# RWKV heads on one core: both triangular masks in one operation, token shift shared with ScalarE, key norms in two halves, some steps in another place

## The chip, the core and the metric

One NeuronCore of a Trainium2 chip runs the whole program. Its engines are TensorE (PE; PEld is its weight load), VectorE (DVE), ScalarE (ACT), GpSimd (POOL) and SyncE (SP, which issues most DMAs). Each engine works through its own list of instructions in the order written, and waits at an instruction until the semaphores that it names have been raised. The metric is device time in microseconds (us), lower is better.

## What is computed

Two model blocks run one after the other on 256 tokens of width 1024. The first has two layers of feed-forward, mixer, feed-forward; the second has attention, a pooling mixer and two mixtures of experts and is not touched. The change lies in the RWKV half of the first block's mixer, 8 heads of 64, once in each layer:

```python
def token_shift(p, mu):
    prev = jnp.pad(p, ((0, 0), (1, 0), (0, 0)))[:, :-1]
    return p + mu * (prev - p)

def rwkv7_group(p, mu, ...):
    p = token_shift(p, mu)
    r, k, v, w_d, a_d, g_d = jnp.split(p, [o1, o2, o3, o4, o5], axis=-1)
    log_w = -jax.nn.softplus(-(w0 + jnp.tanh(w_d) @ w_lora_up).astype(f32)) - 0.5
    decay = jnp.exp(-jnp.exp(log_w))
    a = jax.nn.sigmoid((a0 + a_d @ a_lora_up).astype(f32))
    kk = heads(k * k_k)
    kk = kk * lax.rsqrt(jnp.maximum(jnp.sum(kk * kk, axis=-1, keepdims=True), 1e-24))
    k_h = heads(k.astype(f32) * (1.0 + (a - 1.0) * k_a.astype(f32)))
    y = rwkv7_scan(r_h, heads(decay), k_h, v_h, -kk, kk * a_h)
    ...

def step(state, inp):          # of rwkv7_scan, over the tokens
    sa = jnp.einsum('bhvk,bhk->bhv', state, a_t)
    state = state * w_t[:, :, None, :] + sa[..., None] * b_t[:, :, None, :] + v_t[..., None] * k_t[:, :, None, :]
    return state, jnp.einsum('bhvk,bhk->bhv', state, r_t)
```

## The kernel before

Nothing is scheduled automatically: the order of the Python code is the order on every engine. Activations lie with features on the partitions and 256 tokens along the row. A weight slab of 1 MB comes by DMA, is cut into a high half (ScalarE, L111) and a remainder (VectorE, L117), and a projection of 128 features is `linear_half` (L607): 8 times three matmuls, high weights by high input (L530), high weights by low input (L531), low weights by high input (L532), 24 in all. The third needs what L117 made. `W.next()` hands out the weights of one such unit and at the same moment writes the L111 and L117 of the unit two places further on into the lists of ScalarE and VectorE; `cuts(3)` does so for up to three units at once.

In `mix_body` the scan over tokens is done in chunks of 64 by matmuls. It has these parts.

- `elementwise(hp)` (L800) is a generator for the pair of head blocks hp (0 or 1). Its steps, cut by `yield`: key projection, first half; key projection, second half, with the token shift of the keys and their squares (L819); receptance projection, first half; second half, then the norms of the keys (matmuls L829, `rsqrt` with its power on GpSimd, L595, tile nk), the decay matmuls L838 with the activations L845 to L862 and the scan L851, and the shift of r; then the matmuls L783 that spread nk over the partitions, and the products kn, AR, BK up to bon (L890); value projection in two halves; last a matmul with bon (L902), for hp 0 after four small matmuls of `warm` (L523).
- `shift` (L767) makes p from the projection (L771), the difference d of neighbours (L773) and p + mu d (L776, once for each half of 128 features).
- `matrices(q)` (L914) works on one block of two heads: products L931, masks L943 and L946 (strictly upper part into G or Gk, upper part with diagonal into R), the first step of an inverse on GpSimd (L967, L968: tile Tt), transposes L955 and L957 with ScalarE's copies L958 to L963, products L973 and transposes L979 with ScalarE's copies L975 and L981, transposes L986 with copies L988 into Tm, then ten rounds in which PE (L1005) and VectorE (L1011 to L1017) take turns, and the rest of the scan.
- `lockstep` (L1206) advances two `matrices` generators by a step each per round, and between rounds takes steps from a third generator that fills in projections. AT1 (L422) lists the rounds after which a fill step is taken: `[0, 0, 1, 1, 2, 2, 3, 4, ...]`. For the first pair the fill is `elementwise(1)` followed by `ret_qk`, and all of `elementwise(0)` runs ahead of it (L1233 to L1237).

PSUM has 8 banks: `bank()` hands out four in turn, `abank()` the other four. A matmul that starts on a bank waits until the last reader of that bank's tile from four calls earlier has finished. In `matrices` the calls of two heads in step are: L931 of the first head two banks, of the second head two, L955 one each, L973 and L979 two each, L986 one each. So L986 of the first head takes the bank that its own L973 filled and that ScalarE's L975 reads, and L986 of the second head takes the bank that the first head's L979 filled and L981 reads.

Of the kernel before, what the change touches and what calls it, by code (L numbers as in the profile page):

```python
# [18 lines left out]
P = 128  # L19
T = 256  # L20
# [313 lines left out]
def _c1():  # L334
# [4 lines left out]
    i, t64 = j % 64, q[None, :]  # L339
    parts = {"strict": i < t64, "incl": i <= t64, "level1": (t64 == i + 1) & (i % 2 == 0), "eye": i == t64}  # L340
    for m in (2, 4, 8, 16, 32):
# [79 lines left out]

AT1 = [0, 0, 1, 1, 2, 2, 3, 4, 14, 15, 17, 18]  # L422
AT2 = [0, 1, 2, 3, 4, 5, 6, 7, 8, 9, 10, 11, 14, 15, 17, 99]
# [9 lines left out]
def body(ctx, tc, nc, A, out):  # L433
# [153 lines left out]
    def rsqrt(out, src, scale, eps, work, floor=None):  # L587

        n = src.shape[-1]
        v = work.tile([P, 16], F32, name="nv", bufs=1)[:, :n]  # L590
# [150 lines left out]
    def mix_body(l, xs, nxt, mx):  # L741
# [11 lines left out]

        Gs = [mat.tile([P, 4, 64], F32, name=f"G{i}") for i in range(2)]
        Qs = [mat.tile([P, 4, 64], F32, name=f"Q{i}") for i in range(2)]
# [11 lines left out]
        def shift(pool, name, blk, pb, **kw):  # L767

            p = ew.tile([P, 2, T + 1], F32, name="p")
            nc.gpsimd.memset(p[:, :, 0:1], 0.0)  # L770
            nc.vector.tensor_tensor(p[:, :, 1:], two(pb), by2(rr), op=OP.mult)  # L771
            d = ew.tile([P, 2, T], F32, name="d")
            nc.vector.tensor_tensor(d, p[:, :, :T], p[:, :, 1:], op=OP.subtract)  # L773
            s = pool.tile([P, 2, T], F32, name=name, **kw)
            for j in range(2):
                nc.vector.scalar_tensor_tensor(s[:, j, :], d[:, j, :], vec("shift_mu", l, blk + j), p[:, j, 1:],  # L776
                                               op0=OP.mult, op1=OP.add)
            return s
# [21 lines left out]
        def elementwise(hp):  # L800
# [30 lines left out]
            nk = ew.tile([P, 8], F32, name="nk")  # L831
            rsqrt(nk, pk[:, :8], None, None, ew, floor=1e-24)

# [80 lines left out]
        def matrices(q):  # L914
            hp, i = divmod(q, 2)
            S = H[hp]
            AR, BK, ec, v = S["AR"][:, :, i], S["BK"][:, i], S["ec"][:, i], S["v"][:, i]
            G, Q = Gs[i], Qs[i]
            lo, hi = slice(0, 64), slice(64, P)
# [16 lines left out]
            for w in range(2):  # L936
                nc.gpsimd.tensor_copy(vx[:, :, 1 - w], vw[:, :, w])
            Gk = tile_([P, 4, 64], "Tm")
            R = tile_([P, 4, 2, 64], "R")
            pgs = [p.rearrange("p (t w x e) -> p t w x e", t=2, w=2, x=2) for p in pgs]  # L940
            for dst, r, w in ((G, lo, 0), (G, hi, 1), (Gk, lo, 1), (Gk, hi, 0)):
                for s in range(2):
                    nc.vector.tensor_tensor(dst[r, 2 * s:2 * s + 2], pgs[s][r, :, w, 0],  # L943
                                            cst["strict"][r, None, :].to_broadcast([64, 2, 64]), op=OP.mult)
            for s in range(2):
                nc.vector.tensor_tensor(R[:, 2 * s:2 * s + 2], pgs[s][:, :, :, 1],  # L946
                                        cst["incl"][:, None, None, :].to_broadcast([P, 2, 2, 64]), op=OP.mult)
            yield
# [17 lines left out]
            Tm = tile_([P, 4, 64], "Tm")  # L966
            nc.gpsimd.tensor_tensor(Tt, G, cst["level1"][:, None, :].to_broadcast([P, 4, 64]), op=OP.mult)  # L967
            nc.gpsimd.tensor_tensor(Tt, Tt, cst["eye"][:, None, :].to_broadcast([P, 4, 64]), op=OP.add)  # L968
            yield
            pz = abank()  # L970
            for n, (s, t) in enumerate(ST):
                for a, b in ((lo, hi), (hi, lo)):
                    nc.tensor.matmul(pz[a, n * 64:(n + 1) * 64], Gk[b, n, :], Vt[b, t, 64 * s:64 * s + 64],  # L973
                                     start=(n == 0), stop=(n == 3), skip_group_check=True)
# [16 lines left out]
            for lev in range(5):  # L991
# [1583 lines left out]
```

## Time and profile before

| | us |
|---|---|
| time, median of 3 (lowest, highest) | 2116.79 (2116.5, 2120.3) |
| profiled execution, its own time | 2116.78 |
| its span, first to last instruction | 2115.0 |
| PE busy in the span | 2016.1 (95%) |
| VectorE, ScalarE, GpSimd busy | 1067.3, 803.0, 284.9 |

The mixer of layer 0 lies at about 204 to 412 us, that of layer 1 at about 806 to 1014. A row of the timeline gives the start, the time until the last of its merged instructions ended, engine, line, operation, what it writes and reads, the count, and in brackets how long the engine had been idle before and who ended that. The granted clock (PEclk) is 1.00 at TensorE's upper level of 2.4 GHz and 0.50 at its lower of 1.2. Ends of matmuls are modelled, so starts are the firmer numbers.

### The profile page before, as it was taken

The page shows a single profiled execution, that of the slowest core. Times are in us where ns is not written, and L with a number is a line of the kernel's source. Part 1 is how long each engine was busy: PE and PEld are TensorE (multiplying, and loading weights), DVE is VectorE, ACT ScalarE, POOL GpSimd, SP SyncE. Part 2 cuts the span into 40 slices and gives each one's busy share as a digit, 9 for nine tenths or more (in the row PEclk, how much of TensorE's full clock was granted, in tenths as well). Part 3 has the DMA queues.
Part 4 walks back from the last instruction along what each step waited for, and adds up shares of the span by engine and source line. Part 5 has one row for each costly group of instructions (what it writes and reads, how often), then busy time and mean ns, then how long its engine had stood idle before and what let it go on. Part 6 is the DMA issues. An engine that isn't in the chain of part 4 may idle for free. (4 is left out here: it accounts for less than half of the span.)

```text
span 2115.0 us, 39279 instructions
## 1 busy us (share of the span) xinstructions
PE 2016.1 (95%) x16724; PEld 1692.6 (80%) x16724; DVE 1067.3 (50%) x1680; ACT 803.0 (38%) x1306; POOL 284.9 (13%) x376
## 2 busy tenths in 40 slices
PE   8999999999999999899999998999999898999996
PEld 8999888899999999878999997997444398864442
DVE  5555764555565556754656567645211266441112
ACT  5444442454454445332444454443111244421111
POOL 3111221111121112221111122300000012000000
PEclk9999999999999999999999999999999999999998
DMA  6445321145545554210544443447999935389995
GB/s 257 185 180 183 129 80 61 61 170 189 187 154 199 190 188 170 81 61 22 214 170 183 180 152 115 180 147 308 416 421 421 404 131 208 131 342 420 421 421 246
DMA packets 63499, 442.98 MB, mean 209 GB/s; under 512 B 6993, under 2 KB 7761, under 8 KB 10705
## 3 DMA queue, kind: packets, MB, share of 16 engines
q1 hardware_dynamic: 60704, 433.30, 53.2%
q10 hardware_dynamic: 1744, 3.90, 0.6%
q0 software_dynamic: 864, 3.15, 0.5%
q8 instruction: 136, 2.23, 0.4%
q14 instruction: 51, 0.41, 0.1%
HBM read 439.27 MB, written 1.05 MB: 208 GB/s over the span
## 5 line engine op out<-in xcount | busy, mean ns | idle before, releaser
L117 DVE TENSOR_TENSOR w<-raw,w 128x1024 fp32r<-128x1024 f32 (+1 forms) x428 | 521.1, 1242 | 228.8 <-ACT w L111 228.5
L530 PE MATMUL pb<-xh,w 128*128 128x256 f32 x2032 | 588.7, 290 | 4.1 <-ACT w L111 3.3
L532 PE MATMUL pb<-xh,w 128*128 128x256 f32 x2032 | 582.2, 287 | 8.1 <-DVE w L117 7.9
L531 PE MATMUL pb<-xl,w 128*128 128x256 f32 x2032 | 582.0, 286 | 7.0 <-DVE xl L1408 4.6
L111 ACT ACTIVATE w<-raw 128x1024 fp32r<-128x1024 f32 (+1 forms) x438 | 443.8, 1046 | 197.7 <-PE pb L532 108.7
L532 PEld LDWEIGHTS pb<-xh,w 128*128 128x128 f32 x2032 | 395.2, 194 | 11.4 <-DVE w L117 11.3
L531 PEld LDWEIGHTS pb<-xl,w 128*128 128x128 f32 x2032 | 395.5, 195 | 10.7 <-DVE xl L1408 5.1
L530 PEld LDWEIGHTS pb<-xh,w 128*128 128x128 f32 x2032 | 395.4, 195 | 10.2 <-ACT w L111 3.8
L532 PE MATMUL ab<-hh,w 128*128 128x256 f32 x704 | 197.9, 281 | 0.0
L530 PE MATMUL ab<-hh,w 128*128 128x256 f32 x704 | 197.9, 281 | 0.0
L531 PE MATMUL ab<-hl,w 128*128 128x256 f32 x704 | 196.3, 279 | 0.0
L2247 PE MATMUL pb<-raw,turn 128*64 128x512 f32 x712 | 175.5, 596 | 0.0
L663 POOL TENSOR_TENSOR h<-sg,gu 128x256 f32<-128x256 f32 x88 | 80.9, 920 | 610.2 <-ACT sg L661 610.2
L530 PEld LDWEIGHTS ab<-hh,w 128*128 128x128 f32 x704 | 132.5, 188 | 0.2 <-issue 0.2
L531 PEld LDWEIGHTS ab<-hl,w 128*128 128x128 f32 x704 | 132.6, 188 | 0.0
L532 PEld LDWEIGHTS ab<-hh,w 128*128 128x128 f32 x704 | 132.2, 188 | 0.0
L2247 PEld LDWEIGHTS pb<-raw,turn 128*64 128x64 f32 x712 | 53.5, 137 | 96.2 <-issue 94.4
L659 DVE TENSOR_TENSOR gu<-pb,rr 128x512 f32<-128x512 f32 x88 | 60.7, 691 | 127.5 <-PE pb L532 121.3
L661 ACT ACTIVATE sg<-gu 128x256 f32<-128x256 f32 x88 | 36.7, 418 | 207.7 <-DVE gu L659 207.7
L2251 ACT ACTIVATE s<-pb 128x512 f32<-128x512 f32 x32 | 19.1, 597 | 199.2 <-PE pb L2247 199.2
L2278 DVE SCALAR_TENSOR_TENSOR ol<-pb,ws,ol 128x512 fp32r<-128x512 f32 x16 | 12.0, 751 | 147.7 <-ACT ol L2277 147.7
L2273 PE MATMUL pb<-raw,h 128*64 128x512 f32 x368 | 85.1, 593 | 0.0
(558 smaller groups left out, 3125.5 us busy)
## 6 DMA issues: line engine op xcount, KB each, us to landing
raw<-in_wpack_dram SPq DMA_DIRECT2D x353, 1024.0 KB, 6.3
w<-in_wpack_dram SPq DMA_DIRECT2D x44, 1024.0 KB, 16.5
x<-in_wpack_dram SPq DMA_DIRECT2D x13, 1024.0 KB, 17.7
gb<-in_vecs_dram POOLq DMA_DIRECT2D x6, 512.0 KB, 7.4
C<-in_c_dram SPq DMA_DIRECT2D x1, 1041.0 KB, 15.5
xin<-in_x_dram SPq DMA_DIRECT2D x2, 512.0 KB, 5.2
mem<-in_mem_dram ACTq DMA_DIRECT2D x1, 1024.0 KB, 9.5
out_dram<-xout SPq DMA_DIRECT2D x4, 256.0 KB, 2.1
```

The source lines that it names most:

```text
L111: self.nc.scalar.activation(h, src, AF.Copy)
L117: (self.nc.gpsimd if pool else self.nc.vector).tensor_tensor(lo, src, h.bitcast(F32), op=OP.subtract)
L530: nc.tensor.matmul(o, wh, xh, start=first, stop=False, skip_group_check=True)
L531: nc.tensor.matmul(o, wh, xl, start=False, stop=False, skip_group_check=True)
L532: nc.tensor.matmul(o, wl, xh, start=False, stop=last, skip_group_check=True)
L659: nc.vector.tensor_tensor(gu, two(pb), rr[:, None, :].to_broadcast([P, 2, T]), op=OP.mult)
L661: nc.scalar.activation(sg, gu[:, 0, :], AF.Silu)
L663: nc.gpsimd.tensor_tensor(h, sg, gu[:, 1, :], op=OP.mult)
L2247: nc.tensor.matmul(o, x_e, w[:, k, :], start=(c == 0), stop=(c == KD - 1), skip_group_check=True)
L2251: nc.scalar.activation(s, pb, AF.Copy)
L2273: nc.tensor.matmul(pb[64 * n:64 * n + 64], h[:, 2 * r + k, :], w[:, k, n * 512:(n + 1) * 512], start=(r == 0 and k == 0), stop=(r == 1 and ...
L2278: V_.scalar_tensor_tensor(o[:, 1], pb, wss[e], o[:, 0].bitcast(F32), op0=OP.mult, op1=OP.subtract)
```

## The change

- `shift`: VectorE's difference d is gone. ScalarE writes d = (1 - mu) p, one activation for each half of 128 features, and VectorE adds mu times the neighbour. The factors 1 - mu are made once at the start by GpSimd.
- `matrices`: one VectorE operation per bank of 512 columns multiplies with both masks side by side; its result GR replaces G, Gk and R. Where 10 operations stood for a head block, 2 stand now. GpSimd's first step on Tt takes its input in two instructions of 64 partitions in place of one of 128.
- The keys' norms: `rsqrt` is called for the two token halves apart.
- The first key projection of `elementwise(1)` is issued ahead of the last step of `elementwise(0)`, and the two fill steps of round 2 move to round 3, the later two by a round each.

```diff
-    parts = {"strict": i < t64, "incl": i <= t64, "level1": ...
+    parts = {"both": np.concatenate([i < t64, i <= t64], axis=1), "level1": ...
-AT1 = [0, 0, 1, 1, 2, 2, 3, 4, 14, 15, 17, 18]
+AT1 = [0, 0, 1, 1, 3, 3, 4, 5, 14, 15, 17, 18]
...
+    vmu = b1.tile([P, 28], F32, name="vmu")
+    nc.gpsimd.tensor_scalar(vmu, vcol[:, mu:mu + 28], -1.0, 1.0, op0=OP.mult, op1=OP.add)
...
-            nc.vector.tensor_tensor(d, p[:, :, :T], p[:, :, 1:], op=OP.subtract)
+            for j in range(2):
+                i = 14 * l + blk + j
+                nc.scalar.activation(d[:, j, :], p[:, j, 1:], AF.Copy, scale=vmu[:, i:i + 1])
...
-                nc.vector.scalar_tensor_tensor(s[:, j, :], d[:, j, :], vec("shift_mu", l, blk + j), p[:, j, 1:],
+                nc.vector.scalar_tensor_tensor(s[:, j, :], p[:, j, :T], vec("shift_mu", l, blk + j), d[:, j, :],
                                                op0=OP.mult, op1=OP.add)
...
-            rsqrt(nk, pk[:, :8], None, None, ew, floor=1e-24)
+            for t in range(2):
+                rsqrt(nk[:, 4 * t:4 * t + 4], pk[:, 4 * t:4 * t + 4], None, None, ew, floor=1e-24)
...
-            for dst, r, w in ((G, lo, 0), (G, hi, 1), (Gk, lo, 1), (Gk, hi, 0)):
-                for s in range(2):
-                    nc.vector.tensor_tensor(dst[r, 2 * s:2 * s + 2], pgs[s][r, :, w, 0],
-                                            cst["strict"][r, None, :].to_broadcast([64, 2, 64]), op=OP.mult)
+            both = cst["both"].rearrange("p (x e) -> p x e", x=2)[:, None].to_broadcast([P, 4, 2, 64])
             for s in range(2):
-                nc.vector.tensor_tensor(R[:, 2 * s:2 * s + 2], pgs[s][:, :, :, 1],
-                                        cst["incl"][:, None, None, :].to_broadcast([P, 2, 2, 64]), op=OP.mult)
+                nc.vector.tensor_tensor(GR[:, s].rearrange("p t w x e -> p (t w) x e"),
+                                        pgs[s].rearrange("p (c x e) -> p c x e", c=4, x=2), both, op=OP.mult)
...
-            nc.gpsimd.tensor_tensor(Tt, G, cst["level1"][:, None, :].to_broadcast([P, 4, 64]), op=OP.mult)
+            for w, r in enumerate((lo, hi)):
+                nc.gpsimd.tensor_tensor(Tt[r], GA[r, :, w], cst["level1"][r, None, :].to_broadcast([64, 4, 64]), op=OP.mult)
...
         together(e0, ret_v(), 7)
+        e1 = elementwise(1)
+        next(e1)
         for _ in e0:
             pass
-        lockstep([steps(matrices(0)), steps(matrices(1))], chained(elementwise(1), qk_steps), AT1)
+        lockstep([steps(matrices(0)), steps(matrices(1))], chained(e1, qk_steps), AT1[1:])
```

Place A, where `elementwise(0)` ends. On PE, of before, the last value projection of `elementwise(0)` is followed by these (L523 is `warm`, L902 the matmul with bon, L931 the first products of the two head blocks, L530 to L532 the key projection of `elementwise(1)`; "..." leaves out the equal rows):

```order
L523 LDWEIGHTS identb
L523 MATMUL pb<-identb 128x512
...
L902 MATMUL pb<-r_2740,bones 128x512
L931 MATMUL ab<-AR,BK 128x128 x16
L530 MATMUL pb<-xh,w 128x256
L531 MATMUL pb<-xl,w 128x256
L532 MATMUL pb<-xh,w 128x256
```

The same place of after:

```order
L533 MATMUL pb<-xh,w 128x256
L534 MATMUL pb<-xl,w 128x256
L535 MATMUL pb<-xh,w 128x256
...
L526 LDWEIGHTS identb
L526 MATMUL pb<-identb 128x512
...
L907 MATMUL pb<-r_2746,bones 128x512
L936 MATMUL ab<-AR,BK 128x128 x16
```

The 24 matmuls of the first key projection, which stood behind L902 and L931, stand ahead of `warm` and of the matmul with bon.

On VectorE at the same place, of before (L890 makes bon; the two L117 are the remainders for the two key projections of `elementwise(1)`; L771 to L776 the value shift; then masks):

```order
L890 SCALAR_TENSOR_TENSOR r_2740<-r,vcol,k 128x256 x2
L117 TENSOR_TENSOR w<-raw,w 128x1024 x2
L771 TENSOR_TENSOR p<-pb,rr 128x2x256
L773 TENSOR_TENSOR d<-p 128x512
L776 SCALAR_TENSOR_TENSOR v<-d,vcol,p 128x256 x2
L903 TENSOR_TENSOR r_2740<-pb,v 128x512
L943 TENSOR_TENSOR G_2338<-ab,C_94 64x128 x4
...
L946 TENSOR_TENSOR R_2854<-ab,C_94 128x256 x2
L117 TENSOR_TENSOR w<-raw,w 128x1024 x3
```

and of after:

```order
L895 SCALAR_TENSOR_TENSOR r_2746<-r,vcol,k 128x256 x2
L117 TENSOR_TENSOR w<-raw,w 128x1024 x2
L773 TENSOR_TENSOR p<-pb,rr 128x2x256
L780 SCALAR_TENSOR_TENSOR v<-p,vcol,d 128x256 x2
L117 TENSOR_TENSOR w<-raw,w 128x1024
L908 TENSOR_TENSOR r_2746<-pb,v 128x512
L949 TENSOR_TENSOR GR_2863<-ab,C_94 128x512 x2
L949 TENSOR_TENSOR GR_2879<-ab,C_94 128x512 x2
L117 TENSOR_TENSOR w<-raw,w 128x1024 x2
```

One of the three later remainders has moved ahead of the masks, 20 masks have become 4, and the remainders for the two key projections stand, as before, behind bon.

Place B, two rounds later. On PE, of before (L838 the decay matmuls, L973 and L979 of both head blocks, L783 the spreading of nk, L986 the transposes that lead to Tm; "..." is a projection):

```order
L838 MATMUL pb<-lo,LORA 128x256 x4
L973 MATMUL ab<-Vt_2936,Tm_2828 64x64 x8
L979 MATMUL ab<-ident,BK 128x128 x4
L973 MATMUL ab<-Vt_2952,Tm_2853 64x64 x8
L979 MATMUL ab<-ident,BK 128x128 x4
L783 MATMUL pb<-ident,nk 64x128 x8
...
L986 MATMUL ab<-C_94,Tt_2948 64x64 x8
L986 MATMUL ab<-C_94,Tt_2964 64x64 x8
```

and of after:

```order
L843 MATMUL pb<-lo,LORA 128x256 x4
L979 MATMUL ab<-Vt_2926,GR_2863 64x64 x8
L985 MATMUL ab<-ident,BK 128x128 x4
L979 MATMUL ab<-Vt_2943,GR_2879 64x64 x8
L985 MATMUL ab<-ident,BK 128x128 x4
L992 MATMUL ab<-C_94,Tt_2938 64x64 x8
L992 MATMUL ab<-C_94,Tt_2955 64x64 x8
L787 MATMUL pb<-ident,nk 64x128 x8
```

L783 (now L787) and the value projection behind it have moved past L986 (now L992), which follows L979 (now L985) directly.

On ScalarE at place B, of after (L853 to L867 are L848 to L862 of before with the new d, L777, between; L981 and L987 are L975 and L981 of before, L994 the copy into Tm):

```order
L853 ACTIVATE lw<-lw 128x512
L859 ACTIVATE ec<-cs 128x8x64
L861 ACTIVATE lw<-cs 128x512
L777 ACTIVATE d<-p,vmu 128x256 x2
L865 ACTIVATE d<-a,vneg,vka 128x256 x2
L867 ACTIVATE a<-a 128x512
L981 ACTIVATE AZ_2928<-ab 128x4x64
L987 ACTIVATE BKt_3078<-ab 128x512
```

But for the two L777 the order on ScalarE is that of before: the copies out of PSUM stand behind the activations of the receptance step.

## Rows read from the trace of the kernel before

**Rows 1.** PE's longest waits, 204 to 345 us: waiter <- releaser: total us, times, longest
```profile
PE pb L783 <- POOL nk L595: 2.7, 1, 2.7
PE pb L532 <- DVE w L117: 2.0, 2, 1.7
```

**Rows 2.** Timeline of PE, layer 0, place A
```profile
246.92 1.04 PE L523 MATMUL pb<-identb 128*128 128x512 bf16 x4
...
249.62 1.13 PE L902 MATMUL pb<-r,bones 128*128 128x512 f32 x2 [1.66 <-DVE r L890]
...
253.12 0.28 PE L530 MATMUL pb<-xh,w 128*128 128x256 f32 x1
...
255.52 0.28 PE L532 MATMUL pb<-xh,w 128*128 128x256 f32 x1
...
261.53 0.39 PE L532 MATMUL pb<-xh,w 128*128 128x256 f32 x1 [1.74 <-DVE w L117]
```

**Rows 3.** Timeline of PE, layer 0, place B
```profile
268.02 1.13 PE L838 MATMUL pb<-lo,LORA 64*128 64x256 f32 x8
...
270.90 0.66 PE L979 MATMUL ab<-ident,BK 128*128 128x128 f32 x4
...
274.30 1.09 PE L783 MATMUL pb<-ident,nk 128*64 128x128 f32 x16 [2.74 <-POOL nk L595]
...
279.87 1.15 PE L986 MATMUL ab<-C,Tt 64*64 64x64 f32 x32
```

**Rows 4.** Timeline of PE, layer 1, places A and B
```profile
851.73 1.12 PE L902 MATMUL pb<-r,bones 128*128 128x512 f32 x2 [1.67 <-DVE r L890]
...
876.39 1.98 PE L783 MATMUL pb<-ident,nk 128*64 128x128 f32 x16 [2.75 <-POOL nk L595]
```

**Rows 5.** Timeline of VectorE, layer 0, place A
```profile
240.86 0.69 DVE L773 TENSOR_TENSOR d<-p 128x512 f32<-128x512 f32 x1
...
241.58 0.88 DVE L776 SCALAR_TENSOR_TENSOR r<-d,vcol,p 128x256 f32<-128x256 f32 x2
...
249.49 2.34 DVE L117 TENSOR_TENSOR w<-raw,w 128x1024 fp32r<-128x1024 f32 x2
...
254.86 0.99 DVE L943 TENSOR_TENSOR G<-ab,C 64x128 f32<-64x128 f32 x4
...
256.89 0.75 DVE L946 TENSOR_TENSOR R<-ab,C 128x256 f32<-128x256 f32 x2
...
260.26 3.48 DVE L117 TENSOR_TENSOR w<-raw,w 128x1024 fp32r<-128x1024 f32 x3
```

**Rows 6.** Timeline of ScalarE, layer 0, places A and B
```profile
240.74 0.62 ACT L856 ACTIVATE lw<-cs 128x512 f32<-128x512 f32 x1
...
265.75 0.91 ACT L819 ACTIVATE cs<-k,vcol 128x256 f32<-128x256 f32 x2 [8.86 <-DVE k L776]
...
269.22 1.99 ACT L111 ACTIVATE w<-raw 128x1024 fp32r<-128x1024 f32 x2
...
271.12 0.82 ACT L845 ACTIVATE lw<-pb,vhalf 128x256 f32<-128x256 f32 x2
...
276.88 1.09 ACT L860 ACTIVATE d<-a,vneg,vka 128x256 f32<-128x256 f32 x2 [1.21 <-DVE r L776]
...
278.54 0.36 ACT L975 ACTIVATE AZ<-ab 128x256 f32<-128x256 f32 x1
```

**Rows 7.** By line: durations in ns, min/median/max, of all of a form
```profile
L595 POOL TENSOR_TENSOR nk<-nv,minus_half x4: 2544/2553/2557, 236.0 to 873.8; 128x8 f32<-128x8 f32 x4
...
L595 POOL TENSOR_TENSOR ny<-nv,minus_half x8: 1007/1007/1018, 327.6 to 1000.4; 128x4 f32<-128x4 f32 x8
```

**Rows 8.** Stretches: length, busy us of PE, PEld, DVE, ACT, POOL; PEclk; DMA share, GB/s
```profile
250.00:256.00 6.00, 6.00 (x62) 5.21 (x60) 5.71 (x12) 0.16 (x1) 1.31 (x6) 1.00 0.48 175
...
256.00:264.00 8.00, 6.26 (x53) 6.06 (x52) 7.90 (x20) 0.90 (x1) 2.87 (x4) 1.00 0.02 4
...
275.60:279.01 3.41, 3.41 (x18) 3.41 (x18) 2.62 (x6) 2.17 (x6) 0.30 (x1) 0.50 0.03 12
```

More of the change, by code (lines that the diff above doesn't have):

```diff
@@ L339, in _c1 @@
     i, t64 = j % 64, q[None, :]
-    parts = {"strict": i < t64, "incl": i <= t64, "level1": (t64 == i + 1) & (i % 2 == 0), "eye": i == t64}
+    parts = {"both": np.concatenate([i < t64, i <= t64], axis=1), "level1": (t64 == i + 1) & (i % 2 == 0), "eye": i == t64}
     for m in (2, 4, 8, 16, 32):
@@ L505, in body @@
     nc.gpsimd.tensor_scalar(vneg, vcol[:, neg:neg + 8], -0.5, 1.0, op0=OP.mult, op1=OP.add)
+    mu = col["shift_mu"][0]
+    vmu = b1.tile([P, 28], F32, name="vmu")
+    nc.gpsimd.tensor_scalar(vmu, vcol[:, mu:mu + 28], -1.0, 1.0, op0=OP.mult, op1=OP.add)
     vka = b1.tile([P, 8], F32, name="vka")
@@ L589, in rsqrt @@
         n = src.shape[-1]
-        v = work.tile([P, 16], F32, name="nv", bufs=1)[:, :n]
+        v = work.tile([P, 16], F32, name="nv", bufs=2)[:, :n]
         if floor is None:
@@ L752, in mix_body @@
         SBs = [mat.tile([P, 3, P], F32, name=f"SB{i}") for i in range(2)]
-        Gs = [mat.tile([P, 4, 64], F32, name=f"G{i}") for i in range(2)]
         Qs = [mat.tile([P, 4, 64], F32, name=f"Q{i}") for i in range(2)]
@@ L917, in matrices @@
             AR, BK, ec, v = S["AR"][:, :, i], S["BK"][:, i], S["ec"][:, i], S["v"][:, i]
-            G, Q = Gs[i], Qs[i]
+            Q = Qs[i]
             lo, hi = slice(0, 64), slice(64, P)
@@ L937, in matrices @@
                 nc.gpsimd.tensor_copy(vx[:, :, 1 - w], vw[:, :, w])
-            Gk = tile_([P, 4, 64], "Tm")
-            R = tile_([P, 4, 2, 64], "R")
-            pgs = [p.rearrange("p (t w x e) -> p t w x e", t=2, w=2, x=2) for p in pgs]
-            for dst, r, w in ((G, lo, 0), (G, hi, 1), (Gk, lo, 1), (Gk, hi, 0)):
-                for s in range(2):
-                    nc.vector.tensor_tensor(dst[r, 2 * s:2 * s + 2], pgs[s][r, :, w, 0],
-                                            cst["strict"][r, None, :].to_broadcast([64, 2, 64]), op=OP.mult)
+            GR = tile_([P, 2, 2, 2, 2, 64], "GR")
+            both = cst["both"].rearrange("p (x e) -> p x e", x=2)[:, None].to_broadcast([P, 4, 2, 64])
             for s in range(2):
-                nc.vector.tensor_tensor(R[:, 2 * s:2 * s + 2], pgs[s][:, :, :, 1],
-                                        cst["incl"][:, None, None, :].to_broadcast([P, 2, 2, 64]), op=OP.mult)
+                nc.vector.tensor_tensor(GR[:, s].rearrange("p t w x e -> p (t w) x e"),
+                                        pgs[s].rearrange("p (c x e) -> p c x e", c=4, x=2), both, op=OP.mult)
+            GA = GR[:, :, :, :, 0].rearrange("p s t w e -> p (s t) w e")
+            R = GR[:, :, :, :, 1].rearrange("p s t w e -> p (s t) w e")
             yield
@@ L971, in matrices @@
             for n, (s, t) in enumerate(ST):
-                for a, b in ((lo, hi), (hi, lo)):
-                    nc.tensor.matmul(pz[a, n * 64:(n + 1) * 64], Gk[b, n, :], Vt[b, t, 64 * s:64 * s + 64],
+                for w, (a, b) in enumerate(((lo, hi), (hi, lo))):
+                    nc.tensor.matmul(pz[a, n * 64:(n + 1) * 64], GA[b, n, w, :], Vt[b, t, 64 * s:64 * s + 64],
                                      start=(n == 0), stop=(n == 3), skip_group_check=True)
@@ L1004, in products @@
                         for r in (lo, hi):
-                            nc.tensor.matmul(pb[r, n], a[r, n, :], b[r, n], start=(n == 0), stop=(n == 3),
+                            m_ = GA[r, n, r.start // 64, :] if a is None else a[r, n, :]
+                            nc.tensor.matmul(pb[r, n], m_, b[r, n], start=(n == 0), stop=(n == 3),
                                              skip_group_check=True)
                     return pb
-                pq = products(G, half(Tm, 0))
+                pq = products(None, half(Tm, 0))
                 mask = cst[f"level{m}"].rearrange("p (n e) -> p n e", e=m)
```

## The prediction

> **What bounds the kernel now.** I read the totals first: PE is busy for 95% of the span, so the end moves by what PE waits, and by the stretches in which it runs at its lower clock. Next the waits of PE in the stretch that the change touches, and then, for each, the timelines of PE and of the engine that ended it. Three waits bear on the change; each stands once in a layer. The matmul with bon waits 1.66 us for VectorE [rows 2]; the third matmul of the receptance projection waits 1.74 for its remainder, L117 [rows 1, 2]; and L783 waits 2.74 for GpSimd's power that makes nk [rows 1, 3]. Layer 1 shows the first and the last with 1.67 and 2.75 [rows 4]. Behind the last one there is a second loss: from 275.60 to 279.01 PE has a granted clock of 0.50, its lower level, while around the two waits at place A it stays at 1.00 [rows 8]. L986 starts 5.57 after L783 (279.87 - 274.30) [rows 3]. Between them lie eight small matmuls and one projection of 24 at 0.12 each (253.12 to 255.52 is 20 steps) [rows 2], so 1.0 + 2.9 = 3.9 at the upper level. The lower level costs 1.7 there. PE takes its list in order and no other engine is near its load, so I let a us that PE loses here count as one at the end.
>
> **Place A.** The first key projection now stands ahead of `warm` and of the matmul with bon. Its two first matmuls need only the high half of the weights; the third needs the first L117. On VectorE that L117 is not moved: it stands behind bon, as before. Of before the pair of L117 starts at 249.49 and lasts 2.34 [rows 5], so the first ends near 250.7. To this comes the new shift of r: p is ready at 240.86, where the difference starts [rows 5]; ScalarE is in L856 until 241.36 [rows 6], then writes two d at the price of the pair L819, 0.91 [rows 6], to 242.27; half of L776's pair, 0.44, ends it at 242.71 in place of 242.46 (241.58 + 0.88) [rows 5]. VectorE's chain, and so the L117, comes 0.25 later: 250.95. PE reaches the projection at 246.92, where `warm` started [rows 2], does two matmuls, and waits from 247.2 to 250.95, 3.75 us. The waits of 1.66 and 1.74 go, since bon is long ready when PE comes to it, and the receptance projection's L117 is issued ahead of the masks now. So 3.4 becomes 3.75: **+0.3**. The bounds are 0 (ScalarE's d as early as VectorE's was) and +0.5 (both its d one after the other behind another activation).
>
> The clock: 2.74 us of waiting were followed by the lower level in both layers (in layer 1 L783 itself takes 1.98 in place of 1.09 [rows 3, 4]), 1.66 and 1.74 were not [rows 8]. A wait of 3.75 is nearer to the former and longer, so I count a stretch like that of 275.60, whose cost I worked out at 1.7: **+1.7**, with bounds of 0 and 1.7.
>
> **Place B.** L986 (now L992) follows directly on L979 (now L985); nk's spreading and a projection have moved behind it. It writes the bank that ScalarE's copies into AZ read, the first of which starts at 278.54 and lasts 0.36 [rows 6]. Of before that was hidden: L986 starts at 279.87, a us after the copy's end at 278.90. Now PE comes to it when L979 ends, at 270.90 + 0.66 = 271.56 [rows 3], and the copy still stands on ScalarE behind the activations of the receptance step, L845 to L862, which contain two waits, for VectorE's scan and for r [rows 6]. From the start of L845 to the end of the copy is 278.90 - 271.12 = 7.8, and the new d between them add 0.2 by the sum at place A: 8.0. When can it start? L845 waited for ScalarE, which was held up by L819, whose k came late after 8.86 of idling, and then by the L111 of 269.22 [rows 6]. That k stood on VectorE behind 20 masks and three L117 [rows 5]. Masks: for a head block two times 0.99 and 0.75 make 2.7, for two 5.5; now 4 operations of 128x512, and the nearest, L773, takes 0.69 [rows 5], so 2.8 in all, 2.7 less. With the later start I let ScalarE be free 2.5 earlier, near 268.6, and then L838's results decide, 268.02 + 1.13 = 269.15 [rows 3]. The copy ends at 269.2 + 8.0 = 277.2, PE waits 5.6 there in place of 2.74: **+2.9**. The bounds: if ScalarE isn't free before 271.1 the wait is 1.9 longer; if the lists slide so that the copy ends by 271.6, there is none (a rival, below).
>
> nk itself gets faster. The power on 128x8 takes 2.55, on 128x4 1.007 [rows 7], so two halves 2.0, and with the L117 ahead of it out of the way it is ready at about 270.8. L787 comes behind L992 and doesn't wait for it; the gain is already in the exchange of 2.74 for 5.6. [...]
>
> The clock at B: before it cost 1.7. After a wait of 5.6 the lower level should come again, but a part of the stretch may lie in the wait itself. Bounds 0 and 1.7; I take 1.0, nearer to what the 2.74 left: **-0.7**.
>
> **Priced at nothing.** The second pair of head blocks has the same shorter masks, 2.7 us of VectorE; PE works there on what stood before them, and none of its long waits is for a mask [rows 1]. GpSimd's first step on Tt becomes two instructions, at most as long again as one; Tt is wanted two rounds later, at L986. The d on ScalarE elsewhere cost 0.91 a pair and take 0.69 off VectorE; in these shifts ScalarE has idle time such as the 8.86 ahead of L819 [rows 6]. If that cover were gone, a step would be later by the 0.25 above. GpSimd's factors at the start are one small operation, long before their use. The fill steps that moved to later rounds do the same work, between rounds in which PE and VectorE take turns, and may fill a wait or open one; bounds of -0.5 and +0.5 in a layer, and I take 0. The order of SP's transfers is unchanged.
>
> **Sum.** 0.3 + 1.7 + 2.9 - 0.7 = +4.2 us for a layer, +8.4 for two. The profiled execution took 2116.78, beside a median of 2116.79, so the base is 2116.8: **2125.2**. With the clock's stretch at A worth half and none at B it is +2.35 and 2121.5; with ScalarE late (+1.9) and the whole stretch at B (+0.7) +6.8 and 2130.4.
>
> **The rivals.**
> *The waits, but no fall of the clock at A.* The same waits, and PE keeps its upper level behind 3.75 as it did behind 1.66 and 1.74: 0.3 + 2.9 - 0.7 = +2.5, or with no lower stretch at B either +1.5: 2119.8 to 2121.8, mostly within what counts as no change. For it: only one length of wait in the rows draws the lower level. Against it: this wait is longer than that one. The Trainium skill ("TensorE: Matmul & The Clock Gate", section "What's actually happening") has the chip watch activity in windows that don't start with the kernel; by that the same wait may cost the clock in one layer and not in the other, and the sum would be 2123.5. Layers 0 and 1 agree here in the 2.74 [rows 3, 4].
>
> *Faster: nk was the only obstacle.* If ScalarE's copies come out of the way by 271.6, since the receptance chain starts early enough or the copies are not what L992 waits for, then PE runs through L992 into L787, whose nk is there. The wait of 2.74 and its clock's 1.7 go, 4.4 for a layer; with +0.3 at A this is 2116.8 - 8.2 = 2108.6. With the masks' time at A turned into earlier L117 it could go on to 2101 (another 3.75 for a layer). It is decided by one time: the end of the AZ copy, 5.6 earlier than I count. For it: VectorE's load falls, and the wait for nk is the longest in the stretch [rows 1]. Against: the chain L845 to L975 has its own length of 7.8, which the change doesn't shorten, and its start can't be ahead of L838.
>
> *No change.* PE's losses are taken up further on, since the rounds behind B are paced by VectorE, now less loaded, and the waits later in the pair shrink by what these grow: within 2113 to 2119. For it: the later fill steps. Against: PE's share of 95% leaves little waiting to give up.
>
> **How the numbers follow.** About 0.2%, 4.2 us, is what a measurement of this kernel can tell from no change, so faster is below 2112.6 and slower above 2121.0. The forecast has 0.56, nearly all of it slower; the rival without the fall of the clock 0.15, a quarter of it slower; the faster one 0.18; no change 0.11. That is slower 0.60, same 0.22, faster 0.18. The range takes the forecast's bounds but the last bit, both rivals in the middle, and leaves out the faster one and the far end above: 2113 to 2130.
>
> **What would show it.** In the trace after: at place A one wait of PE of about 3.75 at the third matmul of the first key projection (L535), ended by VectorE's L117, none at L907, and a stretch with a clock of 0.50 behind it; at place B a wait of 5 to 6 at L992, ended by ScalarE's AZ copy, and none at L787; nk in two operations of 1.0; GR at about 0.69 each; all of it again some 602 us later. I am wrong if L992 starts within a us of L985, if L117 ends well before 250, or if PE's waits in the rounds behind B fall by several us.

## The result and the profile after

The changed kernel takes 2127.44 us (median; 2124.71 to 2132.13), beside 2116.5 us for the kernel before: a ratio of 1.0063 (of the means, as all ratios here), 95% interval 1.0047 to 1.008, so slower by 0.6%. The forecast was 2125.2 us, range 2113 to 2130. The profiled execution took 2126.82 us (span 2125.0), 10.0 more than the one of before.

PE's waits in the profile after, 204 to 345 us (waiter <- releaser: total us, times, longest):

```profile
PE ab L992 <- ACT AZ L981: 6.7, 1, 6.7
PE pb L535 <- DVE w L117: 3.9, 2, 3.6
```

In place of 1.66, 1.74 and 2.74 us [rows 1, 2, 3] there are two waits, and no other new one of note. The timeline of PE in layer 0, and the same two waits in layer 1:

```profile
250.32 0.39 PE L535 MATMUL pb<-xh,w 128*128 128x256 f32 x1 [3.65 <-DVE w L117]
...
255.46 1.02 PE L907 MATMUL pb<-r,bones 128*128 128x512 f32 x2
...
271.75 0.66 PE L985 MATMUL ab<-ident,BK 128*128 128x128 f32 x4
279.12 1.98 PE L992 MATMUL ab<-C,Tt 64*64 64x64 f32 x32 [6.71 <-ACT AZ L981]
281.02 1.63 PE L787 MATMUL pb<-ident,nk 128*64 128x128 f32 x16
...
856.03 0.58 PE L535 MATMUL pb<-xh,w 128*128 128x256 f32 x1 [3.76 <-DVE w L117]
...
884.59 1.97 PE L992 MATMUL ab<-C,Tt 64*64 64x64 f32 x32 [6.72 <-ACT AZ L981]
```

L907 doesn't wait any more, nor does L787: it follows L992 at once. The granted clock behind the two waits (length, busy time of PE, PEld, VectorE, ScalarE and GpSimd, then PEclk):

```profile
251.40:254.80 3.40, 3.40 (x18) 3.03 (x17) 2.29 (x4) 2.71 (x4) 1.54 (x4) 0.51 0.64 222
279.12:282.10 2.98, 2.98 (x42) 2.86 (x44) 0.00 (x0) 2.46 (x6) 0.00 (x0) 0.50 0.03 5
...
884.59:889.70 5.11, 5.11 (x54) 4.66 (x55) 1.15 (x3) 2.82 (x6) 0.00 (x0) 0.50 0.01 3
```

The lower level stands behind both. In layer 0 it came 1.1 us after PE's restart at A, where before there was none [rows 8]. Behind the wait at B it holds the first 3.0 us in layer 0 and the first 5.1 us in layer 1 (last row): L992 lasts 1.98 in place of 1.15 [rows 3]. What the other engines did there, VectorE first:

```profile
249.05 2.35 DVE L117 TENSOR_TENSOR w<-raw,w 128x1024 fp32r<-128x1024 f32 x2
...
252.71 0.88 DVE L780 SCALAR_TENSOR_TENSOR v<-p,vcol,d 128x256 f32<-128x256 f32 x2 [0.71 <-ACT d L777]
...
257.60 2.48 DVE L949 TENSOR_TENSOR GR<-ab,C 128x512 f32<-128x512 f32 x4 [0.39 <-PE ab L936]
260.00 3.27 DVE L117 TENSOR_TENSOR w<-raw,w 128x1024 fp32r<-128x1024 f32 x2
...
264.58 1.37 DVE L780 SCALAR_TENSOR_TENSOR k<-p,vcol,d 128x256 f32<-128x256 f32 x2 [0.71 <-ACT d L777]
```

ScalarE, from the squares of k to the copy out of PSUM:

```profile
265.10 0.51 ACT L823 ACTIVATE cs<-k,vcol 128x256 f32<-128x256 f32 x1 [0.22 <-DVE k L780]
...
269.07 2.00 ACT L111 ACTIVATE w<-raw 128x1024 fp32r<-128x1024 f32 x2
270.96 0.82 ACT L850 ACTIVATE lw<-pb,vhalf 128x256 f32<-128x256 f32 x2
...
278.60 0.37 ACT L981 ACTIVATE AZ<-ab 128x256 f32<-128x256 f32 x1
```

GpSimd: the first step on Tt (L973, two instructions in a row) and the second (L974) of both head blocks, and nk in halves, all eight of a run (minimum, median, maximum in ns):

```profile
258.97 1.55 POOL L973 TENSOR_TENSOR Tt<-GR,C 64x256 f32<-64x256 f32 x2 [3.48 <-DVE GR L949]
260.60 1.59 POOL L974 TENSOR_TENSOR Tt<-Tt,C 128x256 f32<-128x256 f32 x1
262.16 2.53 POOL L973 TENSOR_TENSOR Tt<-GR,C 64x256 f32<-64x256 f32 x2
264.76 0.91 POOL L974 TENSOR_TENSOR Tt<-Tt,C 128x256 f32<-128x256 f32 x1
...
L598 POOL TENSOR_TENSOR nk<-nv,minus_half x8: 1006/1520/1999, 235.2 to 879.0; 128x4 f32<-128x4 f32 x8
```

Four operations GR take 2.48 us where 20 took 5.5 [rows 5]. But two L117 take 3.27 where a pair takes 2.35, and the halves of nk take between 1.006 and 1.999 us.

**How the time is read in what follows.** The time of a whole execution moves by several us from run to run with the clock. After the second pair's first products (L936) the list of PE is the same in both layers, and yet the stretch to the first spreading of ny takes 66.7 us in layer 0 and 70.3 in layer 1 of the changed kernel, and 63.7 in another kernel (e5_copies_first, below), with a clock of 0.95, 0.88 and 1.00. PE waits about as long in all three (4.1, 3.8 and 4.1 us, the length less PE's busy time):

```profile
336.29:403.00 66.71, 62.64 (x931) 56.85 (x930) 32.67 (x84) 22.12 (x54) 10.49 (x20) 0.95 0.10 34
942.50:1012.79 70.29, 66.53 (x930) 60.89 (x930) 32.63 (x84) 22.11 (x54) 10.54 (x20) 0.88 0.09 32
...
335.32:399.01 63.69, 59.61 (x931) 53.95 (x930) 32.56 (x84) 22.05 (x54) 10.49 (x20) 1.00 0.10 35
```

So beside the ratio I give the length of two stages, from starts of PE in one profile: A from the decay matmuls of the first pair (L838 before, L843 after) to those of the second, B from there to the second pair's first products (L931, L936). For layers 0 and 1, in us:

| kernel | A | B | both, against before |
|---|---|---|---|
| before | 32.4, 32.4 | 63.3, 63.3 | |
| after | 34.0, 33.9 | 67.4, 68.2 | +5.8, +6.3 |
| e1_undo_A | 30.7, 30.8 | 69.3, 69.3 | +4.4, +4.3 |
| e2_undo_B | 33.7, 34.1 | 61.6, 61.6 | -0.4, -0.1 |
| e3_no_moves | 30.7, 30.8 | 63.4, 63.2 | -1.6, -1.8 |
| e4_moves_only | 33.7, 33.7 | 69.1, 69.0 | +7.1, +7.0 |
| e5_copies_first | 33.9, 34.0 | 65.6, 65.6 | +3.9, +3.9 |
| e6_L117_early | 29.5, 29.6 | 69.3, 69.7 | +3.1, +3.5 |
| e7_both_mended | 29.5, 29.6 | 64.7, 66.5 | -1.5, +0.4 |
| e8_no_L117_beside_nk | 32.4, 32.4 | 62.4, 62.4 | -0.9, -1.0 |
| e9_old_B_early_L117 | 29.5, 29.6 | 63.0, 63.0 | -3.2, -3.2 |
| e10_nk_whole | 29.5, 29.5 | 63.0, 63.0 | -3.2, -3.3 |
| e11_copies_first | 29.5, 29.6 | 65.1, 64.5 | -1.2, -1.7 |
| e12_masks_only | 30.9, 30.9 | 63.8, 63.8 | -0.9, -1.0 |

The stages of the changed kernel are 12.1 us longer in sum; the rest of its profiled execution is 2 us shorter than before. Each line comes from one profile, that of e7_both_mended from its longest execution (2116.64 us). The stages tell what the waits and the clock next to them cost, not the whole time: e1_undo_A and e5_copies_first lose 8.7 and 7.7 us in their stages, but by their ratios 2.5 us and nothing. What the rest of the program gave back there is followed up only for e5_copies_first.

### The profile page after: what moved, and what is told of

Read it like the earlier page. It is cut to its first block, busy times and chain, and to the rows that moved or that the text cites. A ratio compares the mean times of both kernels' runs of the same rounds, so it can differ in the third digit from the quotient of the medians.

```text
span 2125.0 us, 39244 instructions
## 1 busy us (share of the span) xinstructions
PE 2017.6 (95%) x16724; PEld 1694.6 (80%) x16724; DVE 1050.1 (49%) x1606; ACT 816.6 (38%) x1334; POOL 299.5 (14%) x389
## 3 DMA queue, kind: packets, MB, share of 16 engines
q8 instruction: 136, 2.23, 0.4%
## 5 line engine op out<-in xcount | busy, mean ns | idle before, releaser
L117 DVE TENSOR_TENSOR w<-raw,w 128x1024 fp32r<-128x1024 f32 (+1 forms) x428 | 524.2, 1250 | 231.6 <-ACT w L111 231.3
L535 PE MATMUL pb<-xh,w 128*128 128x256 f32 x2032 | 579.8, 285 | 12.0 <-DVE w L117 11.9
L535 PEld LDWEIGHTS pb<-xh,w 128*128 128x128 f32 x2032 | 392.4, 193 | 15.0 <-DVE w L117 14.9
L535 PE MATMUL ab<-hh,w 128*128 128x256 f32 x704 | 196.4, 279 | 0.0
L535 PEld LDWEIGHTS ab<-hh,w 128*128 128x128 f32 x704 | 132.3, 188 | 0.0
```

The lines of the kernel that those rows point to most:

```text
L117: (self.nc.gpsimd if pool else self.nc.vector).tensor_tensor(lo, src, h.bitcast(F32), op=OP.subtract)
L535: nc.tensor.matmul(o, wl, xh, start=False, stop=last, skip_group_check=True)
```

## The experiments

The theory: the two moves on PE cost the time, each by one thing that stands late in another engine's list (L117 on VectorE, the copy into AZ on ScalarE). The rival: the arithmetic edits cost it, by more work on ScalarE and GpSimd.

**e1_undo_A and e2_undo_B: one move undone.** Both start from the changed kernel.

```diff
e1_undo_A
-        e1 = elementwise(1)
-        next(e1)
-        lockstep(..., chained(e1, qk_steps), AT1[1:])
+        lockstep(..., chained(elementwise(1), qk_steps), AT1)
e2_undo_B
-AT1 = [0, 0, 1, 1, 3, 3, 4, 5, 14, 15, 17, 18]
+AT1 = [0, 0, 1, 1, 2, 2, 3, 4, 14, 15, 17, 18]
```

> The changed kernel with place A as before (first key projection back behind the matmul with bon), place B as changed. Theory (the two moves on PE cost the time): PE's wait of 3.65 us for L117 at the first key projection goes, the matmul with bon waits 1.7 to 2.0 again, the receptance projection at most 0.5, no lower clock at A, and the wait of 6.7 at the transposes into Tm stays within 1 us. Per layer 3.65 + 1.7 - 1.9 = 3.4 less, so about 2120.6 us. Rival (the arithmetic edits cost it: GpSimd's longer first step on Tt, ScalarE's d): time stays near 2127.

> The changed kernel with the fill steps taken after the rounds of before (place B as before), place A as changed. Theory (the moves): the transposes into Tm no longer wait 6.7 us but under 0.5, because the spreading of nk and a projection stand ahead of them again; the spreading of nk waits 2 to 2.5 us, since both halves of nk took 3.0 us in the changed kernel; the 3.65 us at A stay. Per layer about 4 less: 2119 us. Rival (arithmetic edits): the wait only changes its place, near 2127.

Measured: e1_undo_A 2118.4 us, ratio to the kernel before 1.0012 (0.9996 to 1.0028); e2_undo_B 2114.33 us, 1.0002 (0.9981 to 1.0024). PE's waits, 204 to 345 us, of e1_undo_A:

```profile
PE ab L992 <- ACT AZ L981: 7.8, 1, 7.8
PE pb L907 <- DVE r L895: 1.8, 1, 1.8
```

and of e2_undo_B:

```profile
PE pb L535 <- DVE w L117: 3.9, 2, 3.6
...
PE pb L787 <- POOL nk L598: 1.2, 1, 1.2
...
PE ab L992 <- ACT AZ L981: 0.7, 1, 0.7
```

Each undone move takes its own wait away and leaves the other, as the theory had it; the sizes were expected wrongly. With A undone PE is 3.1 to 3.3 us sooner at the decay matmuls (stage A 30.7 against 34.0) and then stands 1.1 us longer at L992: a part of A's loss is time that ScalarE would otherwise cost at B. So the stages give 1.4 and 2.0 us back, not 3.4. With B undone they give 6.2 and 6.4 back, not 4. There nk was waited for 1.2 us, not 2 to 2.5, for the same reason turned round: the 3.65 us at A let the other engines get ahead (without them, in e3_no_moves below, nk is waited for 2.3).

**e3_no_moves and e4_moves_only: arithmetic or order alone.** The first undoes both moves in the changed kernel (both diffs above), the second makes both in the kernel before.

> The changed kernel with both moves undone: only the masks in one operation, d on ScalarE and nk in halves are left. Theory (the moves): faster than the kernel before, since the receptance projection's wait of 1.74 us for L117 goes with the shorter masks: 2110 to 2114 us, PE waits of 1.7 to 2.0 for bon and 2 to 3.2 for nk. Rival (arithmetic edits cost the time): 2123 to 2127.

> The kernel before with both moves and none of the arithmetic edits. Theory (the moves): as slow as the changed kernel or a little slower, because the long masks make k, and with it ScalarE's copies, later: 2126 to 2131 us, waits of about 3.4 us for L117 at A and 6.5 to 8.5 for the AZ copy at B. Rival (arithmetic edits): near 2117.

Measured: e3_no_moves 2109.0 us, 0.9961 (0.9937 to 0.9984); e4_moves_only 2130.89 us, 1.0077 (1.0047 to 1.0107). The waits of e3_no_moves:

```profile
PE pb L787 <- POOL nk L598: 2.3, 1, 2.3
PE pb L907 <- DVE r L895: 1.8, 1, 1.8
```

and of e4_moves_only:

```profile
PE ab L986 <- ACT AZ L975: 8.0, 1, 8.0
PE pb L532 <- DVE w L117: 3.7, 2, 3.4
```

The rival falls; e3_no_moves is a little under the 2110 to 2114 expected. The arithmetic edits are a gain of 1.6 and 1.8 us in a layer's two stages, the moves alone a loss of 7.1 and 7.0, and the sums, 5.5 and 5.2, are near the 5.8 and 6.3 of the changed kernel. Beside the arithmetic edits A alone costs 1.2 and 1.7 us (e2_undo_B less e3_no_moves), B alone 5.9 and 6.1 (e1_undo_A less e3_no_moves): B is the larger part by far.

**e5_copies_first and e6_L117_early: PE's list kept, another engine's mended.** In the changed kernel, the receptance step gets a `yield` ahead of its activations, so that `lockstep` writes the copies of `matrices` first; ScalarE's list differs in the place of four copies, the lists of PE and VectorE not at all. In e6_L117_early the weights of one unit more are cut at the receptance step of the first pair.

```diff
e5_copies_first
-AT1 = [0, 0, 1, 1, 3, 3, 4, 5, 14, 15, 17, 18]
+AT1 = [0, 0, 1, 1, 2, 3, 3, 4, 5, 14, 15, 17, 18]
...
             cuts(3)
+            if hp == 1: yield
             lw = ew.tile([P, 2, T], F32, name="lw")
e6_L117_early
-            cuts(3)
+            cuts(4 if hp == 0 else 3)
             lw = ew.tile([P, 2, T], F32, name="lw")
```

> The changed kernel with one thing moved: on ScalarE the four copies out of PSUM (AZ and BKt of both head blocks, L981 and L987) stand ahead of the activations of the receptance step instead of behind them. PE's and VectorE's lists are those of the changed kernel. Theory (the wait at B is for the place of these copies on ScalarE): PE's wait of 6.7 us at L992 falls under 0.5; in its place come about 1.0 for nk at L787 and about 2 for Tm, whose copies stay behind the activations, which now start some 2 us later. 4.4 to 5.9 less in a layer, 2116 to 2119 us. Rival (PE reaches L992 too early for any order of ScalarE, as Tt or BK come late): the wait stays above 4.

> The changed kernel with the weights of the early key projection cut one step sooner, so that its L117 stands on VectorE ahead of the scan and of bon. PE's list is that of the changed kernel. Theory (the wait at A is for that L117's place): the wait of 3.65 us falls under 0.3, the matmul with bon waits under 0.5, no lower clock at A; since PE then reaches B sooner and ScalarE doesn't, the wait at L992 grows to 7.5 to 8.5. 3.5 to 5 less in a layer, 2117 to 2120 us. Rival: the matmul with bon takes the wait over, 2 us and more, and the time falls by less than 4 us.

Measured: e5_copies_first 2112.02 us, 0.9996 (0.9979 to 1.0013); e6_L117_early 2118.6 us, 1.0023 (1.0007 to 1.0038). The waits of e5_copies_first, then its ScalarE at B, and last the clock behind the wait for Tm:

```profile
PE pb L535 <- DVE w L117: 3.9, 2, 3.6
PE ab L1012 <- ACT Tm L994: 2.8, 1, 2.8
```

```profile
271.78 0.37 ACT L981 ACTIVATE AZ<-ab 128x256 f32<-128x256 f32 x1
...
273.84 0.83 ACT L850 ACTIVATE lw<-pb,vhalf 128x256 f32<-128x256 f32 x2
...
281.49 0.64 ACT L994 ACTIVATE Tm<-ab 128x256 f32<-128x256 f32 x2
```

```profile
281.91:288.70 6.79, 6.79 (x55) 6.73 (x56) 5.40 (x10) 1.17 (x2) 2.30 (x3) 0.50 0.01 2
```

The longest wait of e6_L117_early:

```profile
PE ab L992 <- ACT AZ L981: 8.2, 1, 8.2
```

Both mechanisms are shown: with the copies first L992 doesn't wait, with the L117 early A is 4.4 us shorter and neither L535 (0.3 us at most) nor L907 waits. Both also show what is next: Tm's copy (L994), which stands behind the activations, now begun 2.0 us later behind the decay matmuls (4.1 in place of 2.1); and at B the time won at A is in part waited out, so that the stages of e6_L117_early won 2.6 and 2.8 us, not 3.5 to 5. The expectation for e5_copies_first was wrong in the stages too, which won 1.9 and 2.4 us, not 4.4 to 5.9: in layer 0 PE starts the first products of the inverse (L1012) 4.6 us sooner after the decay matmuls, but behind the wait for Tm it runs at its lower level for 6.8 us, in the changed kernel only until 282.1, and 2.7 us of the 4.6 are gone by the second pair's products. Its whole time fell by more, about 14 us by the ratios. Of the 18 us between the two profiled executions 9.6 lie in the stretch from the second pair's products to ny, which takes 63.7 us in both layers here, 66.7 and 70.3 in the changed kernel. Why the clock stays up there, and whether it does in its other executions, no run here shows.

**e7_both_mended: both in one kernel.** It has the edits of e5_copies_first and of e6_L117_early.

> The changed kernel with both: the copies first on ScalarE and the early L117. Theory (the moves cost time by these two places in other engines' lists alone): both long waits gone, 2104 to 2111 us, faster than the kernel before and about as fast as the arithmetic edits alone (2109). Rival (the waits only change hands): 2114 and more.

Measured: 2105.68 us, 0.9969 (0.9952 to 0.9986), faster than the kernel before by 0.3%, as the theory had it; of that its profile shows 1.1 us in the stages of both layers together. Its waits at B are 0.6 for AZ, 0.9 for nk and 2.2 for Tm. That last one is the same in both layers, 2.23 us, and has two endings: stage B takes 64.7 us in layer 0 and 66.5 in layer 1. The rows of layer 1, and the clock behind the wait in both layers:

```profile
877.59 1.92 PE L1012 MATMUL ab<-Tm,GR 64*64 64x32 f32 x32 [2.23 <-ACT Tm L994]
...
277.67:284.47 6.80, 5.78 (x111) 5.53 (x112) 5.74 (x11) 1.16 (x2) 2.51 (x4) 1.00 0.01 2
877.40:884.20 6.80, 6.61 (x54) 6.55 (x55) 5.40 (x10) 1.36 (x3) 2.48 (x3) 0.50 0.00 0
```

At an equal wait PE kept its upper level in one layer (111 matmul rows in 6.8 us) and had the lower in the other (54).

**e8_no_L117_beside_nk: what the power costs.** The kernel before, with one cut fewer in the second pair's receptance step.

```diff
-            cuts(3)
+            cuts(3 if hp == 0 else 2)
             lw = ew.tile([P, 2, T], F32, name="lw")
```

> The kernel before, with the second of the two L117 that surround nk's step taken later, behind the second pair's bon, so that VectorE runs none while GpSimd makes nk. One theory (GpSimd's power is lengthened by VectorE's L117 beside it): nk on 128x8 takes about 1.6 us in place of 2.55 and PE's wait at L783 falls from 2.74 to about 1.8; the later L117 may cost the second value projection 1 to 2. Rival (2.55 is the power's own price for 8 columns): nk takes 2.55 and PE waits 2.74.

One execution took 2112.45 us, too little to tell a difference in time by. GpSimd's nk of the first and of the second pair, PE's wait for it (1.83 in both layers, to 274.06 and 870.75), and the clock behind it:

```profile
236.62 2.55 POOL L595 TENSOR_TENSOR nk<-nv,minus_half 128x8 f32<-128x8 f32 x1 [10.84 <-DVE nv L594]
...
272.36 1.65 POOL L595 TENSOR_TENSOR nk<-nv,minus_half 128x8 f32<-128x8 f32 x1 [11.53 <-DVE nv L594]
```

```profile
PE pb L783 <- POOL nk L595: 1.8, 1, 1.8
```

```profile
274.70:278.00 3.30, 3.30 (x22) 2.97 (x17) 3.13 (x7) 2.06 (x5) 0.00 (x0) 0.50 0.48 201
872.00:875.40 3.40, 3.40 (x17) 3.40 (x17) 2.64 (x6) 2.16 (x6) 0.27 (x1) 0.50 0.30 125
```

The power on 8 columns takes 1.65 us where VectorE runs no L117, and still 2.55 in the first pair, where it does. The 2.55 on which the prediction counted [rows 7] held 0.9 us of standing aside.

**e9_old_B_early_L117, e10_nk_whole, e11_copies_first: a better kernel.** The changed kernel with B undone, and in the receptance step

```diff
-            cuts(3)
+            cuts(4 if hp == 0 else 2)
```

e10_nk_whole makes nk in one operation again; e11_copies_first adds the `yield` of e5_copies_first, with one entry 2 more in AT1 for it.

> The changed kernel with place B as before, with the early key projection kept but its L117 ahead of the scan, and with the L117 that VectorE ran beside GpSimd's nk in the second pair taken later. Theory: no wait at A, none or under 0.5 us for nk at L787 (first half 1.0 in place of 1.99), 1.5 to 2.5 for the AZ copy at L992; from the decay matmuls of the first pair to the second pair's products 91.5 to 93 us, where the kernel before takes 95.7: 2102 to 2109 us, faster than the kernel before. Rival (waits change hands): 94 and more in that stage, 2110 to 2117.

> As e9_old_B_early_L117, but nk made in one operation of 128x8 again. Theory (without an L117 beside it the power on 8 columns takes 1.65): ready 0.35 us sooner than in two halves of 1.0; the same time within what can be measured. Rival (halves help PE to start): L787 waits 0.5 us or more longer.

> As e9_old_B_early_L117, with ScalarE's copies out of PSUM ahead of the receptance activations. Theory: the wait of 1.5 to 2.5 us for the AZ copy at L992 goes, but Tm's copies still stand behind activations that start 1.5 to 2 us later, so half or more of it comes back as a wait at the first round of the inverse: 0 to 1 us less in a layer. Rival: it all comes back, no difference.

Measured: e9_old_B_early_L117 2108.17 us, 0.9967 (0.995 to 0.9983); e10_nk_whole 2104.69 us, 0.9958 (0.9943 to 0.9972); e11_copies_first 2112.66 us, 0.9998 (0.9975 to 1.0021). The longest wait of e9_old_B_early_L117:

```profile
PE pb L787 <- POOL nk L598: 1.7, 1, 1.7
```

The two stages take 92.5 us, as expected, and the kernel beats the one before by 0.3%; but the waits are not those that I named. PE is 4.2 to 4.5 us sooner at the decay matmuls than in e2_undo_B, so nk is waited for 1.7 us, and by the time of L992 the copy is done. nk in one piece or two makes no difference in the stages (92.4 and 92.5), although PE waits 2.4 us for the one piece and 1.7 and 0.4 for the two. The copies first lose here: there is no wait for AZ to win, and the second pair's matmul with bon then waits 2.1 us in layer 0 and 0.6 in layer 1.

**e12_masks_only: which arithmetic edit.** The kernel before with GR in place of G, Gk and R and with the two instructions of GpSimd that GR needs.

> The kernel before with the masks in one operation alone (and GpSimd's first step on Tt in two instructions, which the new layout needs). Theory (of the arithmetic edits the masks bring the gain, by the L117 that stand behind them): the wait of 1.74 us for L117 goes, 1.66 for bon and 2.7 for nk stay; 93.5 to 94.5 us in the stage from the decay matmuls to the second pair, 2109 to 2114 us, as fast as the three edits together. Rival (GpSimd's longer work beside VectorE's L117 eats it up): the L117 wait stays above 1, 2115 and more.

Measured: 2113.36 us, 0.9991 (0.9976 to 1.0006), no difference that can be told; the stages take 94.7 us, 0.9 to 1.0 less than before and a little more than the 93.5 to 94.5 expected. Its longest waits, and the three L117 behind the masks:

```profile
PE pb L782 <- POOL nk L595: 3.3, 1, 3.3
PE pb L901 <- DVE r L889: 1.7, 1, 1.7
```

```profile
257.50 4.95 DVE L117 TENSOR_TENSOR w<-raw,w 128x1024 fp32r<-128x1024 f32 x3
```

The wait of 1.74 for L117 is gone, but PE arrives sooner at nk and waits 3.3 there in place of 2.7, and the three L117 take 4.95 us in place of 3.48 [rows 5]. So the masks are somewhat over half of what the arithmetic edits win in the stages (0.9 to 1.0 of 1.6 to 1.8); what the other two edits add was not split further.

## Why the prediction was right, step by step

**Place A: right.** The wait at L535 is 3.65 and 3.76 us, forecast 3.75, ended by L117 as it was forecast, and L907 and the receptance projection don't wait. The first L117 of the pair starts at 249.05 and PE goes on at 250.32. The clock fell with it in both layers, in layer 1 already at the restart (L535 takes 0.58 there, 0.39 in layer 0). Stage A is 1.5 to 1.6 us longer; the sum had +2.0. e6_L117_early shows the cause: the same list on PE without that wait is 4.4 us shorter. The wait of 1.74 for the receptance projection's L117 goes by either change alone, by the move in e4_moves_only and by the masks in e12_masks_only; I had put it down to the move.

**Place B: right in kind, too small.** The wait is 6.71 us, forecast 5.6. The chain on ScalarE was sized right: from L850's start at 270.96 to the end of the AZ copy at 278.97 is 8.0, as worked out. Its start failed. I let ScalarE be free 2.5 us earlier against the decay matmuls, and it was 1.0: L850 starts 2.1 us behind L843 (268.88), where before it was 3.1 [rows 3, 6] and I had counted 1.15. The masks did save more than counted (2.48 for four in place of 2.8), and VectorE gave it back at once: the two L117 behind them took 3.27 in place of 2.35, and the pair that ends k 1.37 in place of 0.88. That is 1.4 us, more than the 0.9 by which L850 came too late.

**The step that failed is under "Priced at nothing".** GpSimd's first step on Tt in two instructions was given cover. Tt itself had it: it is ready at 265.7, long before L992. Its neighbour had not. Before, Tt was made while VectorE made masks, which read one operand from PSUM. With the masks 3 us shorter, and L973 twice as long, GpSimd's work falls beside VectorE's operations that read two operands from SBUF, and both take longer: L974 1.59 us, L117 0.9 more in the pair, and 0.5 more in the pair that ends k, which has L974 of 264.76 beside it. That pair doesn't owe its length to ScalarE's d: the value shift of the same kernel, with the same wait of 0.71 for d and no Tt beside it, takes 0.88. e12_masks_only, which has the masks and Tt alone, shows the effect on L117 larger (4.95 against 3.48 for three). No run moves Tt to another place, so that ScalarE would else have been free in time is worked out from these rows, not tested. The Trainium skill ("SBUF — State Buffer", section "Who interferes with whom") says that a VectorE instruction with two SBUF inputs contends with a GpSimd instruction that reads SBUF, and one with a single SBUF input, outside VectorE's two-port modes, does not. The trace agrees in both halves: Tt beside the masks of before took 0.73 (minimum, median and maximum of the first step below, of before and then of after), beside L117 1.6 and more.

```profile
L967 POOL TENSOR_TENSOR Tt<-G,C x4: 732/734/739, 255.9 to 337.3; 128x256 f32<-128x256 f32 x4
...
L973 POOL TENSOR_TENSOR Tt<-GR,C x8: 717/739/1711, 259.0 to 343.8; 64x256 f32<-64x256 f32 x8
```

**nk in halves: wrong, and without effect on the sum.** I priced 2.0 us from the row of ny [rows 7]; the two took 3.0, later than in one piece. e8_no_L117_beside_nk shows that the 2.55 in one piece was 1.65 and a wait for VectorE's L117, and the halves keep that wait: their maximum of 1.999 is 1.007 and 1.0 more. The row of ny was the price without the neighbour, the row of nk the price with it, and I compared the two. Nor did an L117 get out of its way: nk was ready at 274.6, not at about 270.8. It cost nothing here because L787 comes 9 us behind L985.

**The clock: -0.7 at B should have been near 0.** Behind the wait the lower level lasted 3.0 us in layer 0 and 5.1 in layer 1; at half the clock that is an estimated loss of 1.5 and 2.5 us, where before it cost 1.7. With that, B's sum is 2.9 + 1.1 - 0.2 = 3.8 in layer 0, where the stage has 4.2, and 2.9 + 1.1 + 0.8 = 4.8 in layer 1, where it has 4.8. So layer 1 is dearer by the clock, and the moved fill steps, priced at 0 with bounds of 0.5, have at most 0.4 left to account for; no experiment looked at them alone.

**The rivals.** The faster one is refuted by its own time: the AZ copy ended at 278.97, not by 271.6. The one without a lower clock at A didn't come about. But the length of a wait does not decide by itself, as I had read from three waits: 1.66 to 1.85 us at place A were not followed by the lower level, 1.83 in e8_no_L117_beside_nk, for nk at B, was in both layers, and the same wait of 2.23 us in e7_both_mended cost the clock in one layer and not in the other. The Trainium skill ("TensorE: Matmul & The Clock Gate", section "What's actually happening") has the activity watched in windows that don't start with the kernel, which is how equal waits can end differently; no run here shows the windows themselves.

**The sum.** +8.4 was forecast; the stages have +12.1, the profiled execution +10.0, the medians +10.9 and the means +13.3. That the median came within 2.2 us of the forecast is in part luck: the two stages missed by 3.7, with A 0.4 to 0.5 too dear in a layer and B 2.0 and 2.6 too cheap, and the rest of the execution, on which the forecast says nothing, was 2 us shorter in the profile.

## What to carry to other kernels

When a matmul is moved ahead, look up for each of its operands, and for the bank that it writes, where the last instruction that makes it ready stands in its own engine's list: a move on PE alone brings the wait with it, and a one-line move on the other engine can win that back (e5, e6), and both together gave a faster kernel (e7). Making one engine's work shorter shifts what runs side by side: price GpSimd's operations by a row in which VectorE does what it will do beside them. And compare stages between fixed instructions where the clock makes whole executions differ by more than the change does.

## What the runs showed of the hardware that was not expected

- GpSimd's power on 128x8 takes 1.65 us, and 2.55 with VectorE's L117 (two SBUF operands) beside it; an addition on 128x256 0.74 and 1.59; an L117 1.2 alone, 1.6 and 1.75 in the pair beside Tt.
- GpSimd's product on 64 partitions takes as long as that on 128 of the same row length (median 0.74 and 0.73 us): cut by partitions it costs twice.
- One list of PE instructions took 63.7, 66.7 or 70.3 us by the granted clock alone (1.00, 0.95, 0.88). A wait of 2.23 us was followed by the lower level in one layer and not in the other; those of 1.66 to 1.85 at place A were not followed by it, that of 1.83 for nk at place B was (e8_no_L117_beside_nk, both layers).
